# First MLP's down projection with the tokens stationary and 512 weight columns moving

## The chip, the cores and the metric

The kernel runs on one core of one Trainium2 chip. The metric is the device time of one execution in microseconds (us). The kernel before takes 757.49 us (median of 3 runs, 757.40 to 757.63). A core has a matrix engine (TensorE: PE in the profile, PEld its weight loads), a vector engine (VectorE: DVE), a scalar engine (ScalarE: ACT), GpSimd (POOL) and DMA queues; here the loads are issued from SyncE's queue (SP). Each engine takes its instructions strictly in the order in which they stand in its own queue and waits on semaphores for the others.

## The reference

A trunk of two layers over 256 tokens of 1024 features, in float32: an even layer (neighbourhood attention and latent attention side by side) and an odd layer (a mixture of dilated windows). Behind each mixer stands a squared-ReLU MLP with 4096 hidden features, and a final RMSNorm closes it:

```python
for layer in range(DEPTH):
    xn = rms_norm(x, norm_mix[layer])
    x = x + (even_mixer(xn, ...) if layer % 2 == 0 else odd_mixer(xn, ...))
    x = x + sq_relu_mlp(rms_norm(x, norm_mlp[layer]), mlp_w1[layer], mlp_w2[layer])
return rms_norm(x, norm_final)

def sq_relu_mlp(xn, w1, w2):
    return jnp.square(jax.nn.relu(xn @ w1)) @ w2
```

The two MLPs are `mlp0` and `mlp1` below. Each is `xn @ w1` (the up projection), a squared ReLU, and `@ w2` (the down projection, the MLP's second product).

## The kernel before

**The residual.** `x` stays on the chip with features on partitions: eight tiles of 128 features by 256 tokens. Every product is made of reduced-precision parts: an operand is split into a high part (`whi`, or half 0 of `xT` and `h`; a ScalarE copy or activation) and a low part (`wlo`, half 1; a VectorE subtraction), and `mm3` (lines 178 to 181) issues three matmuls, high by high, high by low, low by high. A matmul is a pair on TensorE: a load of the stationary operand (128 by 128) and the moving of the other operand through it, 256, 384 or 512 columns here.

**Weights.** One list of weight tiles runs through the whole kernel. A tile of 128 by 2048 floats is loaded by SP into one of 4 `raw` buffers, then split in four pieces into one of 3 pairs of `whi` and `wlo` buffers. A buffer pair comes free only after the last matmul that reads it.

**An MLP** (`mlp`, lines 339 to 374) takes the 4096 hidden features in 16 steps j of 256. `up(j)` makes 48 matmuls of 256 columns (weights stationary, tokens moving), a ReLU on ScalarE, a product on VectorE, and splits the result into `h`. The down projection of step j follows three ups later and adds to four PSUM banks of 512 columns that stay open over all 16 steps (`acc`). The last two steps, j = 14 and 15, are held back and run bank by bank, so that bank after bank is finished and its follow-up work starts while TensorE is busy with the next.

**Down projection, first MLP** (`onto`, lines 315 to 320, called at line 379): the weight piece is stationary, the 256 tokens move: 48 matmuls of 256 columns for each j. The sums come out with features on partitions, as `x` is kept. **Down projection, second MLP** (`finish`, line 410): the tokens of `h` are stationary and 512 weight columns move: 24 matmuls of 512 columns for each j. The sums come out with tokens on partitions, as the output wants them.

**The hand-over** (`hand_over`, lines 291 to 310) goes bank by bank: the last matmuls of the bank, then VectorE scales the sums by the norm's inverse (line 301, in the first MLP only, with `inv` from `inverse_row`, line 260), adds them to `x` (line 303), and `prepare` (line 224) multiplies by the next norm's gains and splits into `xT`, the next stage's operand: ScalarE makes the high part (line 227), VectorE the low part (line 228), one pair of instructions of 256 tokens for each feature tile. After the last bank come the squares for the next norm (lines 230 to 237), summed over features by a matmul with `mean` (line 243).

**The odd layer** begins with the values of head unit 0 (`value_steps`, line 787): for each of two token tiles of 128, 24 matmuls of 384 columns, tokens stationary, over two weight tiles (halves 0 and 1: feature tiles 0 to 3 and 4 to 7). Then come queries and keys (`qk_steps`, line 812: lines 185 and 186, 16 matmuls a group, three weight tiles of two groups each). Each weight tile's sums are rotated (`rope`, line 831: four small SP transfers that swap halves, then VectorE); the keys of the dilated groups land in `k12` (line 846) and are needed by the scores of line 869. The scores of a unit are interleaved with the queries and keys of the next one.

**What sets the order.** The program is written stage by stage, and a scheduler places the instructions of each engine by its own estimates; the follow-up work of a hand-over has raised priority (`tc.high_priority`), the squares are held until behind it (`tc.issue_after`).

Of the kernel before, what the change touches and what calls it, by code (L numbers as in the profile page):

```python
# [23 lines left out]
P = 128  # L24
D = 1024
# [19 lines left out]
def trunk(ctx, tc, a, out):  # L45
# [178 lines left out]
    def prepare(k, n, xT):  # L224

        hi, lo, gk = *halves(xT[:, k]), gains[:, n * KT + k:n * KT + k + 1]
        return (lambda: nc.scalar.activation(hi, x[:, k, :], AF.Copy, scale=gk).ins,
                lambda: nc.vector.scalar_tensor_tensor(lo, x[:, k, :], gk, hi.bitcast(F32), ALU.mult, ALU.subtract).ins)
# [31 lines left out]
    def inverse_row(s):  # L260

        pr = bank("w")
        nc.tensor.matmul(pr[:, 0:T], mean, s[:, 0:T], start=True, stop=True)
        inv = work.tile([P, T], F32, tag="inv", name="inv", bufs=1)
        nc.vector.tensor_scalar(inv, pr[:, 0:T], EPS, None, ALU.add)
        nc.vector.reciprocal(inv, inv)
        return inv

# [22 lines left out]
    def hand_over(accs, last, n, scale=None):  # L291

        xT = x_pair()
        s = sum_tile()
        for b in range(4):
            last[b]()
            v, acc = x[:, 2 * b:2 * b + 2, :], two(accs[b])
            with tc.high_priority(NORM_PRIO):
                if scale is not None:
                    scaled = scratch([2, T], "scaled")  # L300
                    nc.vector.tensor_tensor(scaled, acc, scale.unsqueeze(1).broadcast_to([P, 2, T]), op=ALU.mult)
                    acc = scaled
                nc.vector.tensor_tensor(v, acc, v, op=ALU.add)
                for f in zip(*(prepare(k, n, xT) for k in (2 * b, 2 * b + 1))):
                    done = [step() for step in f]

        with tc.issue_after(done[0]), tc.issue_after(done[1]):
            for b in range(4):
                add_squares(b, s)
        return xT, s  # L310
# [64 lines left out]

    def mlp_between(mp, xT, s):
        def down(accs, hs):
            def step(j, w, f, fbs=range(8)):
                onto(accs, w, f * D, hs[j][:, f], (j, f) == (0, 0), (j, f) == (15, 1), fbs)
            return step  # L380

        accs, hs, inv, w = mlp(mp, xT, lambda: inverse_row(s), range(14, 16), down)

        def last(b):
            for j in w:
                for f in range(2):
                    down(accs, hs)(j, w[j], f, (2 * b, 2 * b + 1))

        return accs, [lambda b=b: last(b) for b in range(4)], inv

    def finish(mp, xT, s):
# [6 lines left out]

        def mm(acc, hs, j, w, f, t, c0, c1, first, last):
            c = slice(f * D + c0, f * D + c1)  # L400
            mm3(acc, hs[j][:, f, 0, tok(t)], hs[j][:, f, 1, tok(t)], w[0][:, c], w[1][:, c], first, last)

        def down(accs, hs):
            def step(j, w, f):
                for i in range(4):
                    end = tail[0] - 1 if i == 3 else 15
                    mm(accs[i], hs, j, w, f, i // 2, (i % 2) * 512, (i % 2) * 512 + 512, (j, f) == (0, 0), (j, f) == (end, 1))
            return step
# [10 lines left out]
        accs, hs, inv, w = mlp(mp, xT, lambda: inverse_columns(s), tail, down, tokens_first)  # L419
        jf = [(j, f) for j in w for f in range(2)]  # L420
        for j, f in jf:
            for h in range(2):
                mm(accs[h], hs, j, w[j], f, 0, h * 512, h * 512 + 512, False, (j, f) == (15, 1))
# [22 lines left out]
        for i, (c0, c1) in enumerate(((0, 512), (512, 768), (768, D))):  # L446
            acc = bank("w") if i else accs[2]
            for n, (j, f) in enumerate(jf):
                mm(acc[:, 0:c1 - c0], hs, j, w[j], f, 1, c0, c1, i > 0 and n == 0, n == len(jf) - 1)
# [315 lines left out]
    def odd(op, xT, s):  # L765
# [147 lines left out]
        run_all(v0[0::2] + v0[1::2])  # L913
# [27 lines left out]
    xT, s = hand_over(accs, last, 2, scale)  # L941
# [95 lines left out]
```

## Time and profile before

| | |
|---|---|
| time, median of 3 runs | 757.49 us (757.40 to 757.63) |
| the profiled execution's own time | 757.89 us |
| its span, from the first to the last instruction | 756.1 us |
| mean granted TensorE clock | 0.998 |
| TensorE busy | 747.7 us |
| VectorE, ScalarE busy | 520.4 us, 459.9 us |
| first MLP on TensorE | 117.7 to 302.4 us of the span |
| odd layer from there | to about 560 us |

Times in the profile's rows are microseconds from the span's start, durations of single instructions in groups are nanoseconds. A matmul's recorded duration includes the way through the array and overlaps its successor: what a matmul costs in a dense stream is the distance from its start to the next one's start.

### The profile page before, as it was taken

Reading aid. Unit: us, or ns where it says so; the run is one execution under the profiler, and the core shown is the slowest. Engines: PE = TensorE matmul, PEld = TensorE weight load, DVE = VectorE, ACT = ScalarE, POOL = GpSimd, SP = SyncE. Lnnn points to the kernel's source line nnn. Section 1 sums busy time; section 2 is a strip of 40 time slices with the busy share of each in tenths; the row PEclk is TensorE's granted clock in tenths of the full one; section 3 lists DMA queues with packets and bytes.
Section 4 is the critical chain, followed back from the end, with each engine's and each line's share of the span. In section 5 each row is a group of like instructions: output and inputs, shape, how many; then the busy total and the mean of one; then the engine's idle time right before and its main releaser. Section 6 shows DMA issues by size and latency. Waiting matters only on the chain.

```text
span 756.1 us, 13978 instructions
## 1 busy us (share of the span) xinstructions
PE 747.7 (99%) x5514; PEld 694.5 (92%) x5514; DVE 520.4 (69%) x1070; ACT 459.9 (61%) x1020; POOL 9.4 (1%) x22
## 2 busy tenths in 40 slices
PE   8999999999999999999999999999999999999996
PEld 5888899999999999989899899998999999899895
DVE  6788859645555556999777887887758554555564
ACT  6688977435434444848776876867756544553541
POOL 0100000000000000100000000000000000000000
PEclk9999999999999999999999999999999999999999
DMA  8764334554554545565655555556654555455501
GB/s 288 304 224 140 112 112 156 181 189 179 191 176 171 211 140 182 193 205 204 200 190 170 201 179 188 174 168 199 217 201 138 193 183 185 178 195 179 185 27 55
DMA packets 27425, 135.40 MB, mean 179 GB/s; under 512 B 4448, under 2 KB 7008, under 8 KB 14432
## 3 DMA queue, kind: packets, MB, share of 16 engines
q1 hardware_dynamic: 27072, 134.23, 51.4%
q8 instruction: 43, 0.70, 0.4%
q10 hardware_dynamic: 288, 0.28, 0.1%
q14 instruction: 22, 0.18, 0.1%
HBM read 127.16 MB, written 1.05 MB: 170 GB/s over the span
## 4 chain that ended last, share of the span: by engine, by line
PE 96%; DMA 2%; issue 1%; SPq 0%; ACT 0%; DVE 0%; POOLq 0%; POOL 0%
PE acc L179 14%; PE acc L180 14%; PE acc L181 14%; PE acc L185 12%; PE w L179 9%; PE w L180 9%; PE w L181 9%; PE acc L186 6%; PE w L200 2%; PE w L887 1%; PE w L869 1%; PE w L701 1%; DMA raw<-in_w_v 1%; PE acc L902 1%; PE w L715 1%
## 5 line engine op out<-in xcount | busy, mean ns | idle before, releaser
L176 DVE TENSOR_TENSOR wlo<-raw,whi 128x512 fp32r<-128x512 f32 (+3 forms) x488 | 304.6, 662 | 153.1 <-ACT whi L175 152.2
L175 ACT CAST whi<-raw 128x512 fp32r<-128x512 f32 (+3 forms) x488 | 266.1, 600 | 190.1 <-issue 174.2
L180 PE MATMUL w<-xT,whi 128*128 128x256 f32 x528 | 149.3, 283 | 0.0
L181 PE MATMUL w<-xT,wlo 128*128 128x256 f32 x528 | 148.9, 282 | 0.0
L179 PE MATMUL w<-xT,whi 128*128 128x256 f32 x528 | 148.9, 282 | 0.0
L185 PE MATMUL acc<-xT,whi 128*128 128x512 f32 x384 | 137.1, 401 | 0.0
L179 PEld LDWEIGHTS w<-xT,whi 128*128 128x128 f32 x528 | 99.5, 189 | 0.6
L186 PE MATMUL acc<-xT,wlo 128*128 128x256 f32 x384 | 100.0, 281 | 0.0
L180 PEld LDWEIGHTS w<-xT,whi 128*128 128x128 f32 x528 | 99.2, 188 | 0.6
L181 PEld LDWEIGHTS w<-xT,wlo 128*128 128x128 f32 x528 | 99.7, 189 | 0.0
L185 PEld LDWEIGHTS acc<-xT,whi 128*128 128x128 f32 x384 | 69.9, 188 | 12.6
L186 PEld LDWEIGHTS acc<-xT,wlo 128*128 128x128 f32 x384 | 72.2, 188 | 3.8 <-issue 0.2
L179 PE MATMUL acc<-h,whi 128*128 128x256 f32 x256 | 72.6, 284 | 0.0
L180 PE MATMUL acc<-h,whi 128*128 128x256 f32 x256 | 72.5, 283 | 0.0
L181 PE MATMUL acc<-h,wlo 128*128 128x256 f32 x256 | 72.5, 283 | 0.0
L179 PE MATMUL acc<-whi,xT 128*128 128x384 f32 (+2 forms) x160 | 56.6, 353 | 0.7 <-ACT whi L175 0.7
L180 PE MATMUL acc<-wlo,xT 128*128 128x384 f32 (+2 forms) x160 | 55.9, 349 | 0.5 <-DVE wlo L176 0.4
L181 PE MATMUL acc<-whi,xT 128*128 128x384 f32 (+2 forms) x160 | 55.1, 344 | 0.0
L179 PEld LDWEIGHTS acc<-h,whi 128*128 128x128 f32 x256 | 49.1, 192 | 0.0
L181 PEld LDWEIGHTS acc<-h,wlo 128*128 128x128 f32 x256 | 49.1, 192 | 0.0
L180 PEld LDWEIGHTS acc<-h,whi 128*128 128x128 f32 x256 | 49.1, 192 | 0.0
L179 PE MATMUL acc<-whi,h 128*128 128x512 f32 x122 | 48.0, 393 | 0.0
(198 smaller groups left out, 1226.4 us busy)
## 6 DMA issues: line engine op xcount, KB each, us to landing
raw<-in_w SPq DMA_DIRECT2D x64, 1024.0 KB, 4.8
raw<-in_w_oqk SPq DMA_DIRECT2D x24, 1024.0 KB, 4.9
raw<-in_w_ov SPq DMA_DIRECT2D x16, 768.0 KB, 4.3
sw<-qk SPq DMA_DIRECT2D x96, 64.0 KB, 2.0
raw<-in_w_qk SPq DMA_DIRECT2D x4, 1024.0 KB, 11.0
raw<-in_w_oe SPq DMA_DIRECT2D x4, 1024.0 KB, 5.0
raw<-in_w_oo SPq DMA_DIRECT2D x4, 1024.0 KB, 4.9
bias<-in_rpb SPq DMA_DIRECT2D x8, 256.0 KB, 3.9
```

The lines of the kernel that those rows point to most:

```text
L175: a = nc.scalar.copy(hi, src).ins
L176: return a, (eng or nc.vector).tensor_tensor(lo, src, hi.bitcast(F32), op=ALU.subtract).ins
L179: nc.tensor.matmul(o, sh, mh, start=first, stop=False)
L180: nc.tensor.matmul(o, sh, ml, start=False, stop=False)
L181: nc.tensor.matmul(o, sl, mh, start=False, stop=last)
L185: both = lambda: nc.tensor.matmul(o, sh, m.rearrange("p v n -> p (v n)"), start=first, stop=last)
L186: low = lambda: nc.tensor.matmul(o[:, 0:T], sl, m[:, 0, :], start=False, stop=False)
L200: nc.tensor.matmul(o[j], qk[pb, 0, a, ts], qk[pb, 1, b, :], start=n == 0, stop=n == 2)
L701: nc.tensor.transpose(pt[:, b * P:(b + 1) * P], pp[:, b // 2, (b % 2) * P:(b % 2 + 1) * P], ident)
L715: nc.tensor.matmul(pvo[64 * j:64 * j + 64, 0:P], v[:, kk, h * 64:(h + 1) * 64], pts[:, 2 * j + kk, :], start=kk == 0, stop=kk == NT - 1)
L869: nc.tensor.matmul(ss[i, j][rows, T:T + P], d["q12"][:, j, i * P + 64 * c:i * P + 64 * c + 64], d["k12"][:, j, 2 * i + c, :], start=True, ...
L887: nc.tensor.transpose(pt[:, b * P:(b + 1) * P], pp[:, b * P:(b + 1) * P], ident)
```

## The change

In the first MLP the down projection takes the form of the second one. For each step j and each half of its hidden features, `mm_tokens` is called for four banks: bank i holds token tile i // 2 and output columns (i % 2) * 512 to + 512. The three matmuls have a token tile of `h` stationary and 512 weight columns moving. The norm's inverse is now one number per partition, so `inverse_columns` takes the place of `inverse_row`.

The sums now have tokens on partitions, and `x` has features there. So the new `hand_over_tokens` turns each finished bank: ScalarE copies the bank to `y` (tile name `down`) and scales it by the token's inverse; TensorE transposes `y` in four pieces of 128 columns into a fresh bank `pt` (tag `w`); VectorE adds that to the four feature tiles of `x`, for 128 tokens; and `prepare`, now with a token slice, splits four feature tiles of 128 tokens each. Banks 0 and 1 complete token tile 0, banks 2 and 3 token tile 1. To suit this, the values of unit 0 are now computed token tile by token tile (`run_all(v0)`), where before half 0 of both token tiles came first.

```diff
-    def prepare(k, n, xT):
-        hi, lo, gk = *halves(xT[:, k]), gains[:, n * KT + k:n * KT + k + 1]
-        return (lambda: nc.scalar.activation(hi, x[:, k, :], AF.Copy, scale=gk).ins,
-                lambda: nc.vector.scalar_tensor_tensor(lo, x[:, k, :], gk, hi.bitcast(F32), ALU.mult, ALU.subtract).ins)
+    def prepare(k, n, xT, ts=slice(0, T)):
+        hi, lo, gk = xT[:, k, 0, ts], xT[:, k, 1, ts], gains[:, n * KT + k:n * KT + k + 1]
+        return (lambda: nc.scalar.activation(hi, x[:, k, ts], AF.Copy, scale=gk).ins,
+                lambda: nc.vector.scalar_tensor_tensor(lo, x[:, k, ts], gk, hi.bitcast(F32), ALU.mult, ALU.subtract).ins)
...
+    def hand_over_tokens(accs, last, n, inv):
+        xT = x_pair()
+        for i in range(4):
+            t, ks = i // 2, range(4 * (i % 2), 4 * (i % 2) + 4)
+            last[i]()
+            with tc.high_priority(NORM_PRIO):
+                y, pt = scratch([512], "down"), bank("w")
+                nc.scalar.activation(y, accs[i], AF.Copy, scale=column(inv, t))
+                for b in range(4):
+                    nc.tensor.transpose(pt[:, tok(b)], y[:, tok(b)], ident)
+                v = x[:, ks[0]:ks[0] + 4, tok(t)]
+                nc.vector.tensor_tensor(v, pt.rearrange("p (b n) -> p b n", b=4), v, op=ALU.add)
+                for f in zip(*(prepare(k, n, xT, tok(t)) for k in ks)):
+                    done = [step() for step in f]
+        return xT, squares_behind(done)
...
+    def mm_tokens(acc, hs, j, w, f, t, c0, c1, first, last):
+        c = slice(f * D + c0, f * D + c1)
+        mm3(acc, hs[j][:, f, 0, tok(t)], hs[j][:, f, 1, tok(t)], w[0][:, c], w[1][:, c], first, last)
+
+    def make_down(ends):
+        def down(accs, hs):
+            def step(j, w, f):
+                for i in range(4):
+                    mm_tokens(accs[i], hs, j, w, f, i // 2, (i % 2) * 512, (i % 2) * 512 + 512, (j, f) == (0, 0), (j, f) == (ends[i], 1))
+            return step
+        return down
+
     def mlp_between(mp, xT, s):
-        def down(accs, hs):
-            def step(j, w, f, fbs=range(8)):
-                onto(accs, w, f * D, hs[j][:, f], (j, f) == (0, 0), (j, f) == (15, 1), fbs)
-            return step
-        accs, hs, inv, w = mlp(mp, xT, lambda: inverse_row(s), range(14, 16), down)
-        def last(b):
+        accs, hs, inv, w = mlp(mp, xT, lambda: inverse_columns(s), range(14, 16), make_down([15] * 4))
+        def last(i):
             for j in w:
                 for f in range(2):
-                    down(accs, hs)(j, w[j], f, (2 * b, 2 * b + 1))
-        return accs, [lambda b=b: last(b) for b in range(4)], inv
+                    mm_tokens(accs[i], hs, j, w[j], f, i // 2, (i % 2) * 512, (i % 2) * 512 + 512, False, (j, f) == (15, 1))
+        return accs, [lambda i=i: last(i) for i in range(4)], inv
...
-        run_all(v0[0::2] + v0[1::2])
+        run_all(v0)
...
-    xT, s = hand_over(accs, last, 2, scale)
+    xT, s = hand_over_tokens(accs, last, 2, scale)
```

The second MLP's own `mm` and `down` become `mm_tokens` and `make_down`, with the same instructions as before. The scheduler's order moves at three places that the prediction speaks of.

TensorE, from the end of bank 1 (`acc_1891`) into bank 2 (`acc_1892`), in the changed kernel; `w_3349<-ident_87,down_3348` are bank 1's four transposes:

```order
L181 MATMUL acc_1891<-whi_3284,h_3243 128x512
L179 MATMUL acc_1892<-whi_3248,h_3139 128x512
L180 MATMUL acc_1892<-wlo_3249,h_3139 128x512
L181 MATMUL acc_1892<-whi_3248,h_3139 128x512
L179 MATMUL acc_1892<-whi_3248,h_3139 128x512
L180 MATMUL acc_1892<-wlo_3249,h_3139 128x512
L312 MATMUL w_3349<-ident_87,down_3348 128x128 x4
L181 MATMUL acc_1892<-whi_3248,h_3139 128x512
```

Each group of four transposes stands inside the next piece of work: bank 0's behind 4 matmuls of bank 1, bank 1's behind 5 of bank 2, bank 2's behind 6 of bank 3, and bank 3's behind 8 matmuls of 384 columns of the odd layer's first values. Everything behind a group on TensorE stands behind its wait for `y`.

ScalarE's queue over the same hand-over, in the changed kernel (`down` is `y`; the casts of 384 columns split the odd layer's value weights):

```order
L310 ACTIVATE down<-acc,ms 128x512
L227 ACTIVATE xT<-x,gains 128x128 x4
L310 ACTIVATE down<-acc,ms 128x512
L227 ACTIVATE xT<-x,gains 128x128 x4
L310 ACTIVATE down<-acc,ms 128x512
L175 CAST whi<-raw 128x384 x3
L227 ACTIVATE xT<-x,gains 128x128 x4
L310 ACTIVATE down<-acc,ms 128x512
L233 ACTIVATE squares<-x 128x512
L233 ACTIVATE q<-x 128x512
L175 CAST whi<-raw 128x384
```

and before:

```order
L227 ACTIVATE xT<-x,gains 128x256 x2
L233 ACTIVATE squares<-x 128x512
L227 ACTIVATE xT<-x,gains 128x256 x2
L175 CAST whi<-raw 128x384
L227 ACTIVATE xT<-x,gains 128x256 x2
L175 CAST whi<-raw 128x384 x2
L233 ACTIVATE q<-x 128x512 x2
L175 CAST whi<-raw 128x384
L175 CAST whi<-raw 128x512
L227 ACTIVATE xT<-x,gains 128x256 x2
```

So each `y` from bank 1 on stands behind the four `xT` pieces of the bank ahead of it, the last one behind three casts as well.

VectorE in the odd layer's first unit, where the keys `k12` are made, before:

```order
L176 TENSOR_TENSOR wlo<-raw,whi 128x384 x3
L836 TENSOR_TENSOR r_4137<-qk,cosT 128x512
L176 TENSOR_TENSOR wlo<-raw,whi 128x384
L837 TENSOR_TENSOR sw<-sw,sinT 128x512
L846 TENSOR_TENSOR k_0_3790<-r_4076,sw 64x8x64 x2
```

and now:

```order
L193 TENSOR_TENSOR qk<-qk,acc 128x256
L176 TENSOR_TENSOR wlo<-raw,whi 128x512 x3
L193 TENSOR_TENSOR qk<-qk,acc 128x256
L843 TENSOR_TENSOR sw<-sw,sinT 128x512
L176 TENSOR_TENSOR wlo<-raw,whi 128x384
L852 TENSOR_TENSOR k_0_3443<-r_3729,sw 64x8x64 x2
```

The keys are made with less work ahead of them, and the scores that need them (line 869, now 875) have moved up on TensorE as well: they stand 11 matmuls behind the scores of line 200 in place of 25. Elsewhere TensorE's order in the odd layer is the same but for single rows.

More of the change, by code (lines that the diff above doesn't have):

```diff
@@ L258, in inverse_columns @@
         return inv
[L260 to L267, printed above, removed]
     def diagonal(r, t):
@@ L289, in run_all, with squares_behind, hand_over @@
             s()
-    def hand_over(accs, last, n, scale=None):
+    def squares_behind(done):
+        s = sum_tile()
+        with tc.issue_after(done[0]), tc.issue_after(done[1]):
+            for b in range(4):
+                add_squares(b, s)
+        return s
+    def hand_over(accs, last, n):
         xT = x_pair()
-        s = sum_tile()
         for b in range(4):
@@ L298, in hand_over @@
             with tc.high_priority(NORM_PRIO):
[L299 to L302, printed above, removed]
                 nc.vector.tensor_tensor(v, acc, v, op=ALU.add)
@@ L305, in hand_over @@
                     done = [step() for step in f]
[L307 to L310, printed above, removed]
+        return xT, squares_behind(done)
[7 more added lines that the diff above has]
+                nc.scalar.activation(y, accs[i], AF.Copy, scale=column(inv, t))
+                for b in range(4):
+                    nc.tensor.transpose(pt[:, tok(b)], y[:, tok(b)], ident)
[3 more added lines that the diff above has]
+                    done = [step() for step in f]
+        return xT, squares_behind(done)
     def open_accs():
@@ L397, in finish @@
         tail = range(13, 16)
[L399 to L408, printed above, removed]
         def tokens_first(j):
@@ L417, in tokens_first @@
                 nc.scalar.copy(xt[:, t, HALF[h]], pt)
-        accs, hs, inv, w = mlp(mp, xT, lambda: inverse_columns(s), tail, down, tokens_first)
+        accs, hs, inv, w = mlp(mp, xT, lambda: inverse_columns(s), tail, make_down([15] * 3 + [tail[0] - 1]), tokens_first)
         jf = [(j, f) for j in w for f in range(2)]
@@ L422, in finish @@
             for h in range(2):
-                mm(accs[h], hs, j, w[j], f, 0, h * 512, h * 512 + 512, False, (j, f) == (15, 1))
+                mm_tokens(accs[h], hs, j, w[j], f, 0, h * 512, h * 512 + 512, False, (j, f) == (15, 1))
         def residual(t, cs, acc):
@@ L448, in finish @@
             for n, (j, f) in enumerate(jf):
-                mm(acc[:, 0:c1 - c0], hs, j, w[j], f, 1, c0, c1, i > 0 and n == 0, n == len(jf) - 1)
+                mm_tokens(acc[:, 0:c1 - c0], hs, j, w[j], f, 1, c0, c1, i > 0 and n == 0, n == len(jf) - 1)
             v = xt[:, 1, c0:c1]
```

## The prediction

> **What bounds the kernel now.** I read the page's first part, the chain of waits, and then the two MLPs side by side by windows.
>
> ```profile
> PE 747.7 (99%) x5514; PEld 694.5 (92%) x5514; DVE 520.4 (69%) x1070; ACT 459.9 (61%) x1020; POOL 9.4 (1%) x22
> PEclk9999999999999999999999999999999999999999
> PE 96%; DMA 2%; issue 1%; SPq 0%; ACT 0%; DVE 0%; POOLq 0%; POOL 0%
> ```
>
> TensorE sets the end: 96% of the chain that ended last is its own work, at full granted clock. So time is won or lost by what TensorE issues, and by waits put in its queue. The edit lies between 135 and about 340 us of the span. There the windows show how densely matmuls follow one another:
>
> ```profile
> core 0: us, PE busy (x) PEld busy (x) DVE busy (x) ACT busy (x) POOL busy (x), PEclk, DMA share, GB/s
> 135.00:141.18 6.18, 6.18 (x52) 6.12 (x51) 5.54 (x8) 3.18 (x6) 0.00 (x0) 1.00 0.39 159
> 585.00:590.93 5.93, 5.93 (x31) 4.95 (x29) 3.94 (x8) 3.19 (x6) 0.00 (x0) 1.00 0.46 169
> 146.94:152.69 5.75, 5.75 (x50) 5.75 (x49) 3.70 (x6) 3.18 (x6) 0.00 (x0) 1.00 0.46 147
> 290.85:302.38 11.53, 11.53 (x99) 11.53 (x98) 8.66 (x16) 5.42 (x13) 0.00 (x0) 1.00 0.54 201
> 608.36:613.84 5.48, 5.48 (x26) 4.51 (x25) 3.69 (x6) 3.18 (x6) 0.00 (x0) 1.00 0.36 136
> 733.37:745.65 12.28, 12.28 (x56) 10.14 (x55) 6.76 (x11) 4.59 (x10) 0.54 (x1) 1.00 0.00 1
> 302.38:310.70 8.32, 8.32 (x51) 8.32 (x49) 8.32 (x17) 7.78 (x17) 1.85 (x2) 1.00 0.51 173
> ```
>
> The edges are starts of matmuls; the counts in brackets include the ones that overlap an edge. 146.94 to 152.69 is one down step of the first MLP: 48 matmuls of 256 columns, 5.75 us, 0.1198 each. 290.85 to 302.38 is its last two steps: 96 of them, 0.1201 each. 608.36 to 613.84 is the same down step in the second MLP, in the form that the change brings: 24 matmuls of 512 columns, 5.48 us, 0.2283 each; its dense tail, 733.37 to 745.65, has 54 at 0.2274. The columns moved are the same; a matmul twice as wide costs 1.9 times as much.
>
> **The change part by part.** *Down steps j = 1 to 13:* 5.75 becomes 5.48, 13 times: -3.51 us. *The first down step, with the norm's sum ahead of it* (first two rows; the second MLP already uses the columns form): 6.18 becomes 5.93, -0.25. The long reciprocal of the row form goes from VectorE; nothing on TensorE waits for it now, so that is worth nothing more. *The held-back steps:* 96 x 0.1201 = 11.53 become 48 x 0.2274 = 10.92, -0.61. Together -4.37 us.
>
> The Trainium skill, page "TensorE: Matmul & The Clock Gate", section "Back-to-back issue gap", gives an isolated gap of N/2.4 + 2.5 ns, 109.2 for 256 columns and 215.8 for 512; by it the 768 and 384 matmuls would differ by 0.96 us, not 4.37. The windows, with 119.8 and 228.3 ns, disagree.
>
> *Transposes.* The second MLP has the same group of four already, between other matmuls:
>
> ```profile
> 596.58 0.28 PE L181 MATMUL w<-xT,wlo 128*128 128x256 f32 x1
> 596.69 0.60 PE L416 MATMUL w<-ident,x 128*128 128x128 f32 x4
> 597.04 0.47 PE L179 MATMUL acc<-whi,h 128*128 128x512 f32 x1
> 597.36 0.39 PE L180 MATMUL acc<-wlo,h 128*128 128x512 f32 x1
> ```
>
> From 596.69 to 597.36 the group and one matmul of 512 columns take 0.67; less 0.23 for the matmul, a group costs 0.44. Four: +1.76. The dearest group of four transposes in the chain of waits gives the upper end, 4 x 0.57 = 2.28:
>
> ```profile
> 64.75 0.57 PE w L607 x4
> ```
>
> *Waits for y.* A group can only start when ScalarE has scaled the bank. Prices from the groups by line (mean ns of one behind the comma):
>
> ```profile
> L545 ACT ACTIVATE vna<-acc,rstd 128x512 f32<-128x512 f32 x2 | 1.4, 680 | 0.0
> L227 ACT ACTIVATE xT<-x,gains 128x256 fp32r<-128x256 f32 x32 | 14.5, 500 | 9.4 <-DVE x L303 8.5 <-DMA gains<-in_gains 0.9
> L880 ACT ACTIVATE pp<-pp,drz 128x384 f32<-128x384 f32 x32 | 18.6, 610 | 0.0
> L807 ACT ACTIVATE v<-acc,rstd 64x128 f32<-64x128 f32 x32 | 11.6, 364 | 3.6 <-DVE v L804 3.2
> L303 DVE TENSOR_TENSOR x<-acc,x 128x512 f32<-128x512 f32 x8 | 5.1, 682 | 1.0 <-PE acc L181 1.0
> L233 ACT ACTIVATE q<-x 128x512 f32<-128x512 f32 x12 | 7.2, 621 | 0.0
> ```
>
> and from the timeline of the old hand-over:
>
> ```profile
> 293.62 0.28 PE L181 MATMUL acc<-h,wlo 128*128 128x256 f32 x1
> 293.94 0.69 DVE L301 TENSOR_TENSOR scaled<-acc,inv 128x512 f32<-128x512 f32 x1 [0.45 <-PE acc L181]
> 298.27 0.91 ACT L227 ACTIVATE xT<-x,gains 128x256 fp32r<-128x256 f32 x2 [1.45 <-DVE x L303]
> 301.06 0.51 ACT L175 CAST whi<-raw 128x384 fp32r<-128x384 f32 x1 [1.88 <-issue]
> ```
>
> `y` is nearest to L545: a bank of 512, scaled by a column, 0.68. VectorE started 0.04 after bank 0's last matmul ended; I take that for each hand-off. An `xT` piece of 128 tokens is not in the trace: with a column scale 256 elements take 0.50 and 384 take 0.61, so 128 take 0.39, and two follow each other with 0.09 of overlap (0.91 for two), so 0.30 apart; L807, half as many partitions out of PSUM, ran without overlap, 0.375 apart. These are the two ends.
>
> The Trainium skill, page "ScalarE: Activation LUTs", section "What ACT_TABLE_LOAD costs", gives 280 + 0.833 N ns for an activation with one column operand, overlapping by 93 ns: for 128 elements an estimate of 387 and 294 ns apart. The two rows agree, and the sum would be the one with the lower end.
>
> Now walk, from the end of bank 0's last slot as 0. The last matmul drains 0.16 longer (0.39 against 0.23), so `y` 0 runs 0.20 to 0.88; its transposes stand at 4 x 0.227 = 0.91, a wait of 0.0 to 0.05. They are drained 0.60 later (L416), VectorE adds until 2.29, ScalarE makes four pieces until 3.6 or 3.85. Bank 1 ends at 2.73 + 0.44 = 3.2; `y` 1 starts at 3.6 or 3.85, is done at 4.2 or 4.5; its group stands at 3.2 + 5 x 0.227 = 4.35: a wait of 0 or 0.2. The same again for bank 2, whose group stands 6 matmuls deep: 0 or 0.3. For bank 3 ScalarE first has three casts for the odd layer's second value tile, which start when TensorE has left the buffers of j = 14 (as at 301.06 before), then four pieces, and only then `y`: the casts start at 8.0 or 8.2, end 1.35 later, the pieces end at 10.6 or 11.1, `y` 3 at 11.3 or 11.8; its group stands 8 x 0.173 (8.32 / 48 in the last window) behind the end of bank 3, at 11.0 or 11.4. A wait of 0.3 or 0.4. Sum: 0.35 to 0.95. A late `y` is a stationary operand, whose load then lies open too; I take 0.50, and 0 to 1.5 for the range.
>
> *Behind bank 3* the values go on: token tile 0, half 1, then tile 1, half 0, 4.9 us in all, before TensorE needs the last pieces of bank 3. These need, behind `y` 3 on ScalarE, two squares and two casts (at most 0.62 each, L233 and 301.06: 2.4, in which the group and the add fit, 0.60 + 0.68) and four pieces (1.5): 3.9. So that is covered, with 1.0 to spare; if the cover were gone, each us late would be a us on TensorE. The weights of half 1 are now wanted 2.1 earlier; their casts are the three above and are long done. The squares are covered by the last 2.1 of values, as they were. SP issues the same loads; the swap transfers of the first rotations move ahead of a value load, which nothing on the path waits for.
>
> *Keys of unit 0.* Before, the keys came in time to within a tenth or two:
>
> ```profile
> 334.82 0.42 DVE L193 TENSOR_TENSOR qk<-qk,acc 128x256 f32<-128x256 f32 x1 [0.42 <-ACT qk L192]
> 336.64 0.68 DVE L836 TENSOR_TENSOR r<-qk,cosT 128x512 f32<-128x512 f32 x1
> 337.25 0.55 DVE L176 TENSOR_TENSOR wlo<-raw,whi 128x384 fp32r<-128x384 f32 x1
> 337.72 0.68 DVE L837 TENSOR_TENSOR sw<-sw,sinT 128x512 f32<-128x512 f32 x1
> 338.43 1.39 DVE L846 TENSOR_TENSOR k<-r,sw 64x512 f32<-64x512 f32 x2
> 339.54 0.39 PE L185 MATMUL acc<-xT,whi 128*128 128x512 f32 x1
> 339.97 1.09 PE L869 MATMUL w<-k,q 128*64 128x128 f32 x16
> ```
>
> A slot of 0.23 behind 339.54 ends at 339.77; the scores began at 339.97, 0.15 behind the keys: a wait of 0.20. Now they stand 14 matmuls sooner. Seven pairs of lines 185 and 186 take 2.46, since the ten pairs between these two starts take 3.52:
>
> ```profile
> 335.67 0.40 PE L185 MATMUL acc<-xT,whi 128*128 128x512 f32 x1
> 339.19 0.39 PE L185 MATMUL acc<-xT,whi 128*128 128x512 f32 x1
> ```
>
> So they stand at 337.31 by this clock. VectorE's queue now has, behind the sum that ended at 335.24: one product (0.61, as 336.64 to 337.25), one split (0.47), the keys (1.39): 337.70, and 337.85 with the hand-off. A wait of 0.54, which is 0.33 more than before. Bounds: -0.20 (no wait left) to 0.8 (another split ahead).
>
> *Sum:* -4.37 + 1.76 + 0.50 + 0.33 = **-1.78 us** against the profiled execution's 757.89 (span 756.1 and 1.8 around it), 756.11; that execution lies 0.40 above the median of the runs, so I predict 757.49 - 1.78 = **755.7 us**.
>
> **The rivals.** *ScalarE queues the turns.* If all pieces cost as much as the 256-wide ones, 0.50 without overlap, each bank takes 0.68 + 2.0 on ScalarE plus 1.4 of transposes and add, against a bank of 3.2; the walk then gives waits of 0.05, 0.7, 0.7 and 0.85, +0.17 in all with 0.33 for the keys and 0.15 for open loads: 757.7. For it: the bank's chain is a ring, ScalarE to TensorE to VectorE to ScalarE; against it: the overlap of two in the rows. At the upper ends of my own bounds (0.95 waiting, 0.8 for the keys) -0.86 is left: 756.6. I put this case at 756.8.
>
> *All turns are covered.* The groups are placed late enough, and the keys come without a wait: -4.37 + 1.76 - 0.20 = -2.81, 754.7. For it: bank 0 has no wait by my own walk; against it: `y` 3 behind the casts.
>
> *The 13 ns by which a matmul exceeds its columns are paid per column here, and the wide form gains next to nothing* (slower). The place is the down steps, the price 384 matmuls at up to 0.2402, where nothing is saved; with a saving of 0.96 the sum is -0.96 + 1.76 + 0.50 + 0.33 = +1.63, 759.1. It decides from 0.237 us a matmul on. The skill's gap, above, is this case. Against it: 0.2274 to 0.2283 in the same form in the second MLP, with the same waits for weights.
>
> *VectorE comes late into the odd layer* (slower). It is at 90% there:
>
> ```profile
> 311.00:340.00 29.00, 28.96 (x175) 24.92 (x175) 26.19 (x51) 16.57 (x37) 1.07 (x1) 1.00 0.65 206
> ```
>
> It has 2.8 us idle in this window; what it comes in late beyond that shifts the keys, and TensorE with them. To be slower than before by more than can be told it would have to be 6 late at the first values. Against it: the new hand-over gives VectorE less (4 adds and 16 small splits for 8 wide steps and 8 wider splits). Price for 6 late: +1.5, 759.0. That the edit does nothing is out: the order shows 24 matmuls of 512 columns for each step.
>
> **How the numbers follow.** A measurement of this kernel can tell about 0.2%, 1.5 us, from no change: faster means below 756.0. The forecast has 0.45, turns queued on ScalarE 0.28, all covered 0.15, gain per column 0.05, late VectorE 0.07. The forecast's own range, 755.1 to 756.4, lies three quarters on the faster side. Faster: 0.34 + 0.15 = 0.49; slower: 0.09 of the last two; same: 0.42. The range for 8 in 10 takes in all covered and the upper ends of the unknown costs with dearer transposes (-0.86 + 0.52, 757.1): 754.6 to 757.2.
>
> **What would show it.** Right: down steps of 5.45 to 5.55 us in the first MLP; transposes with a record of 0.60 for four and the next matmul 0.35 behind their start; gaps ahead of bank 1's to 3's groups of 0 to 0.4 put down to ScalarE, the largest at bank 3's; the first wait of line 875 for VectorE, about half a us. Wrong: a gap over 1 us anywhere from bank 0 to line 875, an `xT` piece well over 0.40, a stop inside the values, or units 1 to 7 of the odd layer taking longer than they did.

## The result, and the profile after

The changed kernel takes **755.17 us** (median of 7 runs, 754.70 to 755.82) against 757.49 for the kernel before (7 runs, 757.09 to 758.30): a ratio of 0.997 with a 95% interval of 0.996 to 0.9979. That is 2.3 us less; 755.7 was forecast. When both were measured again later, the medians were 757.10 and 755.27, 1.8 us apart, so a difference of two medians holds to about half a us, and the terms of the sum are read from traces. The profiled execution of the changed kernel took 755.61 us with a span of 753.8 (before: 757.89 and 756.1), so the two traces show the same 2.3 us that the times show, and the rest of this section finds them there.

From the page of the changed kernel, busy time of each engine, the granted clock in 40 slices, and the chain that ended last:

```profile
PE 744.5 (99%) x5148; PEld 675.7 (90%) x5148; DVE 515.5 (68%) x1079; ACT 462.6 (61%) x1027; POOL 9.5 (1%) x22
PEclk9999999999999999999999999999999999999999
PE 95%; DMA 2%; issue 1%; DVE 1%; SPq 0%; ACT 0%; POOLq 0%; POOL 0%; DVEq 0%
```

TensorE issues 366 matmuls less in the trace (384 fewer and 16 transposes more should be 368; a record or two can be missing) and is busy 3.2 us less, at the same full clock. It still sets the end. In the chain VectorE rounds to 1% where it rounded to 0; the piece of it that lies near the edit is the keys of unit 0, 332.63 to 335.08, shown further below.

The windows of the changed kernel, with edges at starts of matmuls as before (us, then busy time and instructions of PE, PEld, DVE, ACT and POOL, granted clock, DMA share, GB/s):

```profile
134.82:140.74 5.92, 5.92 (x31) 4.96 (x29) 3.94 (x8) 3.19 (x6) 0.00 (x0) 1.00 0.50 177
146.50:151.99 5.49, 5.49 (x27) 4.51 (x26) 3.70 (x6) 3.19 (x6) 0.00 (x0) 1.00 0.38 143
286.95:299.30 12.35, 12.35 (x61) 10.10 (x60) 6.98 (x17) 7.73 (x20) 0.00 (x0) 1.00 0.51 190
299.30:308.31 9.01, 9.00 (x54) 8.60 (x52) 8.56 (x20) 9.01 (x22) 1.85 (x2) 1.00 0.48 160
308.31:311.95 3.64, 3.64 (x25) 3.28 (x25) 2.89 (x9) 2.76 (x7) 1.09 (x1) 1.00 0.54 191
331.78:346.51 14.73, 14.45 (x102) 12.34 (x102) 13.15 (x33) 10.06 (x27) 0.00 (x0) 1.00 0.66 235
```

The rows are, in order: the norm's sum with the first down step (6.18 before); a later down step (5.75); the held-back steps, now with the groups of banks 0 to 2 in them (11.53); the values of unit 0 with the group of bank 3 (8.32); the second norm's sum with what stands around it; and the stretch from the first scores of unit 0 to the values of unit 1. Side by side with the same stretches of before, cut at the same instructions:

| stretch on TensorE | before | after | difference |
|---|---|---|---|
| up to the first norm's sum (nothing is changed there) | 135.00 | 134.82 | -0.18 |
| from there to the held-back steps (ups unchanged at 5.76) | 155.85 | 152.13 | -3.72 |
| held-back steps, with three groups after | 11.53 | 12.35 | +0.82 |
| values of unit 0, with one group after | 8.32 | 9.01 | +0.69 |
| second norm's sum | 3.78 | 3.64 | -0.14 |
| queries and keys up to the first scores | 19.83 | 19.83 | 0.00 |
| first scores to values of unit 1 | 14.57 | 14.73 | +0.16 |
| the rest of TensorE's work | 396.98 | 397.05 | +0.07 |

These add up to -2.1 us behind the start of the edit and -0.2 ahead of it, where nothing is changed; executions of one kernel differ by more (754.70 to 755.82). The four groups of transposes stand on TensorE like this (start, duration, engine, line, operation, tiles, count; rows of the timeline of the changed kernel around banks 0, 1, 2 and 3):

```profile
290.35 0.39 PE L179 MATMUL acc<-whi,h 128*128 128x512 f32 x1
290.61 0.66 PE L312 MATMUL w<-ident,down 128*128 128x128 f32 x4
291.02 0.48 PE L180 MATMUL acc<-wlo,h 128*128 128x512 f32 x1
291.34 0.40 PE L181 MATMUL acc<-whi,h 128*128 128x512 f32 x1
...
293.84 0.39 PE L180 MATMUL acc<-wlo,h 128*128 128x512 f32 x1
294.07 0.60 PE L312 MATMUL w<-ident,down 128*128 128x128 f32 x4
294.42 0.47 PE L181 MATMUL acc<-whi,h 128*128 128x512 f32 x1
294.74 0.39 PE L179 MATMUL acc<-whi,h 128*128 128x512 f32 x1
...
297.25 0.39 PE L181 MATMUL acc<-whi,h 128*128 128x512 f32 x1
297.48 0.60 PE L312 MATMUL w<-ident,down 128*128 128x128 f32 x4
...
300.52 0.34 PE L180 MATMUL acc<-wlo,xT 128*128 128x384 f32 x1
300.88 0.66 PE L312 MATMUL w<-ident,down 128*128 128x128 f32 x4
301.29 0.42 PE L181 MATMUL acc<-whi,xT 128*128 128x384 f32 x1
301.55 0.34 PE L179 MATMUL acc<-whi,xT 128*128 128x384 f32 x1
```

Bank 1's and bank 2's groups start a plain slot (0.23) behind the matmul ahead of them: no wait. Bank 1's group takes 0.35 to the next matmul's start, and that matmul's own slot is 0.32 in place of 0.23: 0.44 in all. Bank 3's starts 0.36 behind a matmul whose slot is 0.17, so it waited 0.19, and takes 0.41 in place of 0.35; with that the late `y` costs 0.25. At bank 0 the same is 0.03 and 0.06. At both the profile has the load of the stationary operand waiting for ScalarE's `y` (tile `down`, line 310).

### The profile page after: what moved, and what is told of

Same layout as the page of the kernel before. It is cut to its first block, busy times and chain, and to the rows that moved or that the text cites. A ratio compares the mean times of both kernels' runs of the same rounds, so it can differ in the third digit from the quotient of the medians.

```text
span 753.8 us, 13273 instructions
## 1 busy us (share of the span) xinstructions
PE 744.5 (99%) x5148; PEld 675.7 (90%) x5148; DVE 515.5 (68%) x1079; ACT 462.6 (61%) x1027; POOL 9.5 (1%) x22
## 4 chain that ended last, share of the span: by engine, by line
PE 95%; DMA 2%; issue 1%; DVE 1%; SPq 0%; ACT 0%; POOLq 0%; POOL 0%; DVEq 0%
PE acc L179 14%; PE acc L180 14%; PE acc L181 14%; PE acc L185 12%; PE w L179 9%; PE w L181 9%; PE w L180 9%; PE acc L186 6%; PE w L200 1%; PE w L893 1%; PE w L875 1%; PE w L707 1%; DMA raw<-in_w_v 1%; PE acc L908 1%; PE w L721 1%
## 5 line engine op out<-in xcount | busy, mean ns | idle before, releaser
L179 PE MATMUL acc<-whi,h 128*128 128x512 f32 x250 | 98.0, 392 | 0.0
L181 PE MATMUL acc<-whi,h 128*128 128x512 f32 x250 | 97.9, 392 | 0.0
L180 PE MATMUL acc<-wlo,h 128*128 128x512 f32 x250 | 97.7, 391 | 0.0
L181 PEld LDWEIGHTS acc<-whi,h 128*128 128x128 f32 x250 | 46.9, 188 | 9.9
L180 PEld LDWEIGHTS acc<-wlo,h 128*128 128x128 f32 x250 | 47.0, 188 | 9.1
L179 PEld LDWEIGHTS acc<-whi,h 128*128 128x128 f32 x250 | 47.0, 188 | 9.0
L192 ACT COPY qk<-acc 128x256 f32<-128x256 f32 x48 | 17.0, 370 | 30.1 <-PE acc L185 29.6
## 6 DMA issues: line engine op xcount, KB each, us to landing
raw<-in_w_qk SPq DMA_DIRECT2D x4, 1024.0 KB, 11.8
```

The lines of the kernel that those rows point to most:

```text
L179: nc.tensor.matmul(o, sh, mh, start=first, stop=False)
L180: nc.tensor.matmul(o, sh, ml, start=False, stop=False)
L181: nc.tensor.matmul(o, sl, mh, start=False, stop=last)
L192: nc.scalar.copy(dst, o[:, T:2 * T])
```

## The experiments

All runs of the first four share one chip and a kernel before of 757.16 us (16 runs), those of the others one chip and 757.10 (21 runs). Every ratio is against the kernel before.

**Only the width undone.** The tokens stay stationary, the banks are turned as in the change, and each matmul of 512 columns becomes two of 256.

```diff
+        def narrow(acc, hs, j, w, f, i, first, last):
+            for q in range(2):
+                c0 = (i % 2) * 512 + 256 * q
+                mm_tokens(acc[:, 256 * q:256 * q + 256], hs, j, w, f, i // 2, c0, c0 + 256, first and q == 0, last and q == 1)
...
-                    mm_tokens(accs[i], hs, j, w[j], f, i // 2, (i % 2) * 512, (i % 2) * 512 + 512, False, (j, f) == (15, 1))
+                    narrow(accs[i], hs, j, w[j], f, i, False, (j, f) == (15, 1))
```

> The changed kernel with only the width undone: in the first MLP the tokens stay stationary and the four banks, the turns and the norm's column form stay, but each matmul moves 256 weight columns in place of 512 (768 matmuls for 384). My theory, that about 13 ns are paid per matmul whatever its width: 48 x 0.120 = 5.75 us a down step again in place of 5.48, +4.3 us, 759.5 us, slower than the kernel before by 2 (the turns without their gain). Rival, that the price is per column, or that the gain comes from the form (tokens stationary) and not from the width: 755.2, as the changed kernel.

It took 760.07 us (4 runs), ratio 1.0038 (1.0023 to 1.0053), span 758.2. The windows of this kernel, the norm's sum with the first down step and then a later down step:

```profile
134.51:140.71 6.20, 6.20 (x54) 6.20 (x53) 3.94 (x8) 3.19 (x6) 0.00 (x0) 1.00 0.53 180
146.47:152.23 5.76, 5.76 (x51) 5.76 (x50) 3.70 (x6) 3.19 (x6) 0.00 (x0) 1.00 0.40 141
```

The 48 matmuls of 256 cost 5.76 again, 0.120 each, with tokens stationary as with weights stationary. So it is the width that pays, and not which operand is stationary. From the norm's sum (134.51) to the first values (303.67) this kernel needs 169.16 us, the changed one 164.48 (134.82 to 299.30): 4.68 more. Width accounts for 4.39 of it (0.28 in the first step, 13 times 0.27, and 96 x 0.120 less 48 x 0.2274 = 0.60 in the held-back steps). The other 0.3 are small waits: in this form the group of every bank, not only bank 3, comes about 0.10 late, as at bank 1:

```profile
297.45 0.28 PE L179 MATMUL acc<-whi,h 128*128 128x256 f32 x1
297.68 0.66 PE L312 MATMUL w<-ident,down 128*128 128x128 f32 x4
298.09 0.36 PE L180 MATMUL acc<-wlo,h 128*128 128x256 f32 x1
```

The rival in which the 13 ns above the columns are paid per column falls. The Trainium skill, page "TensorE: Matmul & The Clock Gate", section "Back-to-back issue gap", gives that rival its numbers, an isolated gap of N/2.4 + 2.5 ns, from which an estimate of 0.96 us follows for 768 matmuls of 256 columns against 384 of 512; the runs show 4.39, and the measurement decides.

**Each group issued twice.** The same four transposes are written again into the same bank.

```diff
-                for b in range(4):
-                    nc.tensor.transpose(pt[:, tok(b)], y[:, tok(b)], ident)
+                for _ in range(2):
+                    for b in range(4):
+                        nc.tensor.transpose(pt[:, tok(b)], y[:, tok(b)], ident)
```

> The changed kernel with every group of four transposes issued twice into the same bank. My theory, that the turns lie on TensorE's path: 16 more transposes at 0.088 each, +1.4 us, 756.6 us; a group's record grows from 0.60 to 0.95, and the waits ahead of the groups stay within 0.1 of what they were, since VectorE's add comes later by as much as the next bank does. Rival, that the turns are covered by waits that TensorE has anyway: no change, 755.2. Second rival, that the ring ScalarE, TensorE, VectorE sets the hand-over: more than +2.5, with waits over 0.3 ahead of the middle groups.

It took 757.53 us (10 runs), ratio 1.0004 (0.9994 to 1.0013), span 755.7: all of the gain is gone again. In the timeline of this kernel bank 1's group, with no wait ahead of it:

```profile
294.21 0.40 PE L180 MATMUL acc<-wlo,h 128*128 128x512 f32 x1
294.44 1.04 PE L313 MATMUL w<-ident,down 128*128 128x128 f32 x8
295.23 0.47 PE L181 MATMUL acc<-whi,h 128*128 128x512 f32 x1
```

Eight take 0.79 to the next start where four took 0.35: 0.44 for four more, a transpose every 0.11. I had put four more at 0.35, the distance to the next matmul, and had forgotten that this matmul's own slot grows as well. Four times 0.44 is 1.76, and the span grew by 1.9; the values have a new wait besides, of a load at 307.38 for VectorE's low part of a weight tile (0.25 by the profile). So the groups are on the path in full: were they hidden in any part, doubling them would have cost less. The waits ahead of the groups are 0.14 at most (at bank 3). That does not yet show that the ring of ScalarE, TensorE and VectorE has room, since a longer group lengthens the ring and TensorE's own work alike. The changed kernel's trace shows it: there `y` of banks 1 and 2 is done at 293.88 and 297.29, 0.19 before its group starts without a wait.

**No transposes at all.** The untransposed `y` is added to `x`: the turning is the part of the computation that is left out.

```diff
-                for b in range(4):
-                    nc.tensor.transpose(pt[:, tok(b)], y[:, tok(b)], ident)
...
-                nc.vector.tensor_tensor(v, pt.rearrange("p (b n) -> p b n", b=4), v, op=ALU.add)
+                nc.vector.tensor_tensor(v, y.rearrange("p (b n) -> p b n", b=4), v, op=ALU.add)
```

> The changed kernel without the transposes: VectorE adds the scaled bank to x as it is, tokens and features exchanged (so this leaves out a part of the computation, and x is not the reference's from there on); every other instruction stays. My theory: -1.78 for four groups at 0.445, -0.33 for the two waits that the profile of the changed kernel shows ahead of banks 0's and 3's groups, and up to -0.45 more, because the scores of line 875 stand 15 matmuls in place of 11 behind those of line 200 in this kernel's order and their wait may go: 752.6 to 753.1 us. Rival, that the hand-over's chain and not the transposes cost the time: no more than -0.5, 754.7.

It took 753.24 us (4 runs), ratio 0.9945 (0.993 to 0.996), span 751.8: 2.0 less than the changed kernel's, where 0.44 a group and 0.34 of waits would be 2.1. The three stretches do not each give back their share, though. Down step 13 and the held-back steps, without groups, take 16.36 us for 72 matmuls, 0.2272 each, as worked out for the dense stream; but the values take 8.55 and not 8.32, and the wait for the keys does not go, which I had expected of it. The 0.23 in the values lie around a load of weights that waits for ScalarE's cast of a value tile: in this build ScalarE has four pieces and four squares to make just ahead of that cast, and it starts at 301.97. The load, and the rows around the scores of unit 0 (line 873 here):

```profile
302.53 0.19 PEld L179 LDWEIGHTS acc<-whi,xT 128*128 128x128 f32 x1 [0.17 <-ACT whi L175]
...
333.24 0.40 PE L185 MATMUL acc<-xT,whi 128*128 128x512 f32 x1
334.12 1.09 PE L873 MATMUL w<-k,q 128*64 128x128 f32 x16 [0.48 <-DVE k L850]
```

A slot of 0.23 behind 333.24 ends at 333.47: a wait of 0.65, longer than with the transposes, although 16 matmuls stand between the near scores and these and not 11. VectorE has another order in this build: two splits of 384 columns stand between the last sum (330.16) and the product (331.52) that leads to the keys. So the transposes do not make this wait; here it follows from the order in which the scheduler laid out VectorE's queue.

**The order of the values put back.** Half 0 of both token tiles first, as before the change.

```diff
-        run_all(v0)
+        run_all(v0[0::2] + v0[1::2])
```

> The changed kernel with only the order of unit 0's values undone: half 0 of both token tiles first, then half 1 of both. My theory: nothing waits in either order. Token tile 1's half 0 needs bank 2's pieces, which the profile of the changed kernel has ready at 300.8 by its clock, and would be reached at 302.1; bank 3's pieces are ready at 304.5 and wanted for the last 12 matmuls in both orders, at 306.2. So 755.2 us, within 0.3 of the changed kernel, and the wait ahead of bank 3's group stays at 0.2 to 0.3. Rival, that the new hand-over needs token tile 0 first: a wait of 1 us or more inside the values, 756.2 or more.

It took 755.37 us (7 runs), ratio 0.9973 (0.9962 to 0.9985), span 753.7. The values take 9.00, bank 3's group waits as long, and the keys too. With the hand-over of the change either order is covered: this part of the edit is worth nothing that could be measured.

**The changed kernel once more**, beside the next three.

> The changed kernel once more, beside the next three on one chip: 755.2 us, 0.3% under the kernel before.

It took 755.27 us (11 runs), ratio 0.9974 (0.9965 to 0.9983), span 753.5: 1.8 us less than the kernel before beside it.

**The far scores of unit 0 later.** They are split from the near ones and issued behind the third group of queries and keys: 16 matmuls behind the near ones and not 11 (15 rows of the trace, of which one stands for two matmuls).

```diff
+            def far():
+                with tc.issue_after(joins[-1]) if u == 0 else ExitStack():
+                    for i in range(NT):
...
-            return [scores] + [wait] * pause + [f for i in range(NT) for j in range(2) for f in (lambda i=i, j=j: turn(i, j), wait)]
+            head = [near, wait, far] + [wait] * (pause - 2) if u == 0 else [lambda: run_all([near, far])] + [wait] * pause
```

> The changed kernel with only the far scores of unit 0 (line 875) placed later on TensorE: 15 rows in place of 11 behind the scores of line 200, with VectorE's order the same up to the keys. My theory: the 0.45 us that TensorE waited for the keys in the profile of the changed kernel goes, since the slot comes 0.8 us later: -0.3 to -0.45, 754.8 us, and no wait for VectorE's keys is listed. Rival: the wait only moves, to the transposes of unit 0's probabilities, which get 0.8 us less: 755.2, with a wait listed there.

It took 754.99 us (8 runs), ratio 0.9973 (0.9963 to 0.9983), span 753.2. In the trace the wait is gone: the scores follow at a slot and a bit, and the stretch from the near scores to the values of unit 1, 14.73 in the changed kernel's second profile, is 14.38. The rows of this kernel's timeline around the far scores, and its window for that stretch:

```profile
335.15 0.40 PE L185 MATMUL acc<-xT,whi 128*128 128x512 f32 x1
335.47 1.09 PE L882 MATMUL w<-k,q 128*64 128x128 f32 x16
```

```profile
331.55:345.93 14.38, 14.38 (x103) 12.33 (x102) 12.97 (x33) 10.27 (x27) 0.00 (x0) 1.00 0.70 245
```

So the keys' lateness costs 0.35 us on TensorE in the changed kernel. The medians differ by 0.28 in the same direction, and the two intervals cover each other: the times alone cannot tell it.

**The same, and bank 3's `y` on VectorE**, to take the wait at bank 3 away too.

```diff
-                nc.scalar.activation(y, accs[i], AF.Copy, scale=column(inv, t))
+                (nc.vector.tensor_scalar(y, accs[i], column(inv, t), None, ALU.mult) if i == 3 else nc.scalar.activation(y, accs[i], AF.Copy, scale=column(inv, t)))
```

> As the run with the far scores later, and bank 3's scaled copy made by VectorE in place of ScalarE, where it stood behind three casts and four pieces. My theory: the 0.24 us wait ahead of bank 3's group goes as well, 754.5 us, and the four groups cost 4 x 0.445 and nothing else. Rival: VectorE is late with the copy (it has the low parts of bank 2 and two splits there), the wait stays at 0.2 or grows: 754.8 or more.

It took 755.05 us (8 runs), ratio 0.9974 (0.9964 to 0.9984), span 753.0. The rows of this kernel at bank 3's group, at the norm's sum behind the values (line 245 here), and of VectorE's last addition of squares ahead of that sum:

```profile
300.41 0.34 PE L179 MATMUL acc<-whi,xT 128*128 128x384 f32 x1
300.59 0.60 PE L314 MATMUL w<-ident,down 128*128 128x128 f32 x4
300.94 0.42 PE L180 MATMUL acc<-wlo,xT 128*128 128x384 f32 x1
...
307.98 0.39 PE L185 MATMUL acc<-xT,whi 128*128 128x512 f32 x1
308.46 0.58 PE L245 MATMUL w<-mean,squares 128*128 128x1 f32 x4
308.90 0.36 PE L186 MATMUL acc<-xT,wlo 128*128 128x256 f32 x1
...
307.90 0.42 DVE L239 TENSOR_TENSOR squares<-squares 128x256 f32<-128x256 f32 x1
```

The group now starts a slot (0.18) behind its predecessor and takes 0.35: the 0.25 at bank 3 are won. They are lost again 8 us later. The norm's sum no longer stands at the head of the next product but three matmuls into it, and starts 0.48 behind a matmul whose slot is 0.23. From the end of the MLP to the end of the norm's sum this kernel needs 12.72 us (298.84 to 311.56), the changed one beside it 12.67 (299.03 to 311.70). The wait has moved, not gone. VectorE is now the late one: its last addition of squares ends at 308.32, 0.14 ahead of the sum, where in the changed kernel beside it the same addition ends at 307.82, 0.22 ahead of a sum that starts without a wait. VectorE has the copy of `y` (0.74) to make here, and a third split stands between its additions of squares. That moving the copy alone does this was not tried.

**The same price tried on the up projections.** If a matmul costs about 0.011 us beyond its columns (0.2283 less 0.1198 for 256 columns more, 0.1085; 0.1198 less that; by the dense stretches, 2 x 0.1201 less 0.2274, it is 0.013), then other products gain from fewer, wider matmuls too. Here both MLPs' up projections move `x_hi` and `x_lo` side by side, 512 columns, through the weights' high part, and `x_hi` through the low part: two matmuls for three. ScalarE and VectorE add the two halves.

```diff
-                        mm3(pu[:, f * T:(f + 1) * T], w[0][:, c], w[1][:, c], *halves(xT[:, k]),
-                            k == 0 and (f == 0 or j > 0), k == KT - 1 and (f == 1 or j > 0))
-            r = scratch([512], "relu")
-            nc.scalar.activation(r, pu, AF.Relu)
+                        mm2(pus[f], w[0][:, c], w[1][:, c], xT[:, k], k == 0, k == KT - 1)
+            for f in range(2):
+                joined(sums[:, f], pus[f])
...
-            nc.vector.tensor_tensor(h, r, pu, op=ALU.mult)
+            s2 = sums.rearrange("p f n -> p (f n)")
+            nc.vector.scalar_tensor_tensor(h, s2, 0.0, s2, ALU.max, ALU.mult)
```

> The changed kernel with the up projections of both MLPs made of pairs in place of triples: the high weights stationary and both parts of xT moving as one matmul of 512 columns, then the low weights and 256 columns (as lines 185 and 186 do it); the two halves of the sum are joined by ScalarE and VectorE before the squared ReLU. The same columns are moved by two thirds of the matmuls. My theory, a price per matmul: a pair takes 0.3515 (lines 185 and 186), a triple 0.360, so 16 x 0.0085 = 0.14 for each of 32 ups, -4.4 us: 750.8 us. Rival, that the wide form pays only where the weights move, or that the joins make the hidden features late: 755 or more, with waits for h ahead of the down steps.

It took **751.36 us** (4 runs, 750.68 to 752.20), ratio 0.9926 (0.9912 to 0.9939): faster than both kernels, by 3.9 us against the change beside it. An up step in the windows of the changed kernel's second run, and the same of this kernel:

```profile
140.44:146.20 5.76, 5.76 (x49) 5.76 (x48) 2.50 (x4) 2.18 (x4) 0.00 (x0) 1.00 0.68 223
```

```profile
141.31:146.93 5.62, 5.62 (x33) 4.89 (x32) 2.92 (x5) 2.56 (x5) 0.00 (x0) 1.00 0.74 227
564.12:580.97 16.85, 16.85 (x99) 14.69 (x98) 16.42 (x32) 12.11 (x27) 0.00 (x0) 1.00 0.34 120
```

5.62 against 5.76, 0.14 for each of 32 steps, with no wait between them; the last row shows the first three ups of the second MLP (17.28 in the change), where VectorE is at 16.42 of 16.85 us: the extra work still fits, barely. 32 x 0.14 is 4.5. For 16 matmuls less in each step that is 0.009 apiece, somewhat under the 0.011 of the down projection. The profiled execution, the slowest of the four at 752.20, came to its first MLP 1.3 us later than the other (118.54 against 117.24), with TensorE waiting 1.0 for the high part of an early weight tile, so its span of 750.2 is only 3.3 shorter than the 753.5 beside it.

## Why the prediction was right, and where its sizes were off

The time lies 0.5 below the 755.7 forecast, inside the forecast's own range but close to its lower end of 755.1, and the gain is made of the parts that the prediction named. Of the 0.5, 0.2 stand in the traces ahead of the edit and are no merit or fault of the sum. Taken by its own steps:

**The matmuls: right.** *Down steps and first down step*: -3.76 was worked out, -3.72 measured, with 5.49 for a step and 5.92 for the first. *Held-back steps*: 10.92 for 48 matmuls; the kernel without transposes shows them at 0.2272 each, 10.91. The width experiment shows that these terms come from the width: undone, 4.39 is lost.

**The transposes: right.** 0.44 a group was taken from the second MLP's group; 0.44 stands at the groups that do not wait, and four more of them in each group cost 0.44 again.

**The waits for `y`: the mechanism right, the size too large.** 0.50 was taken; it is 0.34, nearly all at bank 3, as the walk said (0.3 or 0.4 there; 0.19, with 0.06 for the late start). ScalarE's rows of the changed kernel show why the lower end held (the last column is idle time before the group, and what ended it):

```profile
289.87 0.69 ACT L310 ACTIVATE down<-acc,ms 128x512 f32<-128x512 f32 x1 [0.92 <-PE acc L181]
292.03 1.28 ACT L227 ACTIVATE xT<-x,gains 128x128 fp32r<-128x128 f32 x4 [1.47 <-DVE x L314]
293.21 0.67 ACT L310 ACTIVATE down<-acc,ms 128x512 f32<-128x512 f32 x1
...
297.73 1.35 ACT L175 CAST whi<-raw 128x384 fp32r<-128x384 f32 x3 [0.44 <-ACT down L310]
298.98 1.27 ACT L227 ACTIVATE xT<-x,gains 128x128 fp32r<-128x128 f32 x4
300.15 0.67 ACT L310 ACTIVATE down<-acc,ms 128x512 f32<-128x512 f32 x1
```

Bank 0 ended its last slot at 289.67. `y` 0 started 0.20 later, as walked, and was done at 290.56, 0.89 (walked 0.88). The next `y` starts 1.18 behind the first of four pieces, so pieces are 0.295 apart: the lower of my two ends, 0.30, and not 0.375. So bank 1's `y` was done at 293.88, before its group could be issued (294.07), and banks 1 and 2 wait for nothing. The Trainium skill, page "ScalarE: Activation LUTs", section "What ACT_TABLE_LOAD costs", has the formula by which such a piece takes 387 ns and starts 294 ns behind the one ahead, an estimate. The trace agrees: 1.28 for four is 0.395 and three times 0.295. At bank 3 the casts started at 8.06 on the walk's clock (8.0 or 8.2), the pieces ended at 10.58 (10.6 or 11.1) and `y` 3 at 11.15 (11.3 or 11.8): the overlap of 0.1 between unlike instructions, which I had left out, is what made 0.3 into 0.2. The group stood at 11.02, as walked (11.0 or 11.4).

**Behind bank 3: right, with more to spare.** The last pieces are ready at 303.97 on ScalarE and 304.56 on VectorE; TensorE wants them at 306.23. That is 1.7 us in hand where 1.0 was forecast, and putting the order of the values back changes nothing.

**The keys of unit 0: the mechanism right, the size of its price too large.** The queue of VectorE was forecast as one product, one split and the keys. That is what ran; the rows of the changed kernel, VectorE first and then TensorE:

```profile
332.63 0.68 DVE L843 TENSOR_TENSOR sw<-sw,sinT 128x512 f32<-128x512 f32 x1
333.23 0.55 DVE L176 TENSOR_TENSOR wlo<-raw,whi 128x384 fp32r<-128x384 f32 x1
333.70 1.38 DVE L852 TENSOR_TENSOR k<-r,sw 64x512 f32<-64x512 f32 x2
```

```profile
334.55 0.39 PE L185 MATMUL acc<-xT,whi 128*128 128x512 f32 x1
335.23 1.09 PE L875 MATMUL w<-k,q 128*64 128x128 f32 x16 [0.28 <-DVE k L852]
```

The keys are done at 335.08 and the scores start 0.15 later, 0.45 behind the end of the slot before (334.78); 0.54 was forecast, against 0.20 before. So the wait is 0.25 longer, not 0.33, and of that the stretch gave back 0.09 further on: +0.16 up to unit 1's values. With the wait taken out, that stretch was 0.35 shorter.

**What the sum did not have.** The second norm's sum costs 0.14 less. Before, its four small matmuls stood one matmul into the next product, at 310.95, and took 0.47 to the next start; now they stand ahead of it, at 308.31, and take 0.38. I had the stretch in view as covered and gave it no term. The profile of before has the load for this sum waiting for VectorE's last squares; that of the changed kernel lists no such wait:

```profile
310.95 0.52 PEld L243 LDWEIGHTS w<-mean,squares 128*128 128x128 f32 x4 [0.24 <-DVE squares L237]
```

So the squares, which the forecast took as covered, were only just in time before. That this is the whole 0.14 was not tried by itself. The kernel with bank 3's `y` on VectorE, in which the sum waits for the squares again, lost as much at that place as it had won at bank 3.

Together, against the forecast's terms: +0.04 for the steps up to the held-back ones, -0.14 for the held-back steps, transposes and waits (+1.51 in the table, +1.65 forecast), -0.17 for the keys, -0.14 for the norm's sum and +0.07 for all the rest are -0.34, which takes the forecast's -1.78 to the -2.12 of the table. The waits and the keys, the terms with the widest bounds, were both taken too large, and no large errors cancelled. Two slips in the working change nothing: by its own figures the keys' wait grows by 0.34, not 0.33, and the price of a late VectorE (6 less 2.8, less 1.78) is +1.4 and 758.9, not +1.5 and 759.0.

**The rivals.** *ScalarE queues the turns*: out, by pieces 0.295 apart and by `y` of banks 1 and 2, done 0.19 before it is used. *All turns are covered*: its 754.7 lies as near to 755.17 as my 755.7, so the time alone does not decide; the trace does, with 0.34 at banks 0 and 3 and a wait for the keys that grew. *The gain is per column*: out, by the width experiment. *VectorE comes late into the odd layer*: out; from the end of the MLP up to the scores of line 875 the profile puts no wait on TensorE down to VectorE, and queries and keys take 19.83 in both.

## What to carry to other kernels

Where TensorE is the bound, count matmuls and not only columns: here 256 columns more cost 0.1085 us, and each matmul about 0.011 beyond that, so halving their number at the same columns was worth 0.27 us in every step, and two for three on the up projections another 3.9 in all. This price is measured between 256 and 512 columns and does not reach further down: a transpose moves 128 columns and costs 0.11, and the norm's sum moves one column for each matmul and costs 0.12 ((0.38 + 0.09) / 4, with what the next matmul takes longer). Every one of these matmuls brings the load of its own 128 by 128 stationary operand, and loads and matmuls were saved together in every run, so which of the two carries the price is not shown. A transpose on the bounding engine was not free here: it was charged its slot (0.11 us) and the waits for what comes before it. Four groups cost 1.76 us, so turning once per bank pays against 0.27 won in each of 13 steps, and turning in every step would not (an estimate from these two numbers). Before shortening a wait of a few tenths, look for the next thing that becomes late: here one such wait taken away showed up again 8 us further on, and another, for the keys, did go.

## What the runs showed that I had not expected

A group of transposes that had to wait costs more than its wait: 0.41 to the next start in place of 0.35, in the changed kernel at banks 0 and 3 and in the width experiment at all four.

ScalarE starts an instruction about 0.10 us before the recorded end of the one ahead also where the two are of different kinds (`y` at 300.15, the pieces recorded until 300.25), and not only within a run of equal ones.

In the narrow form with tokens stationary the groups of all four banks were about 0.10 late, where in the wide form two of four were not late at all. There the scheduler sets the groups of banks 0 to 2 only 7 matmuls of 256 (0.84) behind the end of their bank, where `y` needs 0.89; in the wide form banks 1 and 2 leave it 5 and 6 matmuls of 512 (1.14 and 1.36). Why the scheduler places them so stays open.
